# Low parts of the channel mixer's split weights: an adding DMA on the negated high part, in place of a subtraction on VectorE

## The chip, the cores and the metric

One core of one Trainium2 chip runs the whole program. The metric is the time of one execution in microseconds (us) of device time, lower is better. The engines are named as in the profile: PE (TensorE), with PEld for its weight loads, DVE (VectorE), ACT (ScalarE), POOL (GpSimd) and SP (SyncE), which starts most of the DMAs. The 16 DMA engines move the data of every queue.

## The reference, cut to what matters

The kernel computes one layer of a decoder for 512 prompt tokens and 8 x 8 sample tokens, T = 576 columns in all. Two token mixers (a chunked mLSTM and an RWKV-7 branch) come first, then the channel mixer, then a gated input per layer and the last norm. The change lies in the channel mixer's up projection and in the output of `y`:

```python
h2 = rmsnorm(x, lp['norm2_g'])
u = h2 @ lp['f_up']                                # (1024 -> 2 x 2816)
c, fconv_new = causal_dwconv(fconv, u[..., :D_FF], lp['f_conv_w'], lp['f_conv_b'])
x = x + (jax.nn.gelu(c) * u[..., D_FF:]) @ lp['f_down']

gate = jax.nn.sigmoid(rmsnorm(x, lp['ple_norm_g']) @ lp['ple_gate_w'])
x = x + gate * (pe.astype(x.dtype) @ lp['ple_proj'])
...
y_prompt = rmsnorm(y_p, final_norm_g)
```

All inputs are float32.

## The kernel before

Activations lie with 128 features on the partitions and the 576 tokens in the free dimension, in two halves of 288. A matmul takes a 128x128 weight tile and 128x288 activations. To keep more digits than one float32r pass has, every operand is split in a high part (the value rounded to float32r) and a low part (what is left), and a product is three matmuls: high x high, high x low, low x high. Weights come by DMA as float32 tiles `wr` of 128 x 4 x 128 (256 KB), ACT makes the high part `wh` by a cast (S.copy), and DVE the low part `wl` by a subtraction (wr - wh). For most weights this is done in `wload` (lines 166 and 167).

The up projection of the channel mixer has 22 blocks `j` of 128 gate features and 128 value features. The first three (`lead2`) go through `wload` and `dense`. The other 19 go through `up(j)` and `seven`, which treats gate and value rows, two halves of the inputs and two halves of the tokens as a 2x2 block product and does it with seven products in place of eight. `seven` loads four raw tiles (`wdma8`: a11, a21, a22, a12, in 6 rotating buffers `wr`), forms four sums of weights (`plus`: s1, s2, s4 on DVE, s3 on POOL, in 3 rotating buffers `ws`), and makes seven pairs of parts (`parts`, lines 287 to 290): of a11, s2, s1, a12, s3, a22 and s4. Each pair feeds one `prod` of 4 x 3 matmuls on PE (line 300). The pairs rotate in 4 buffers of `wh` and 4 of `wl`, which the other projections share. The combinations of the products, the convolution (L1333, L1335), the gelu (L1336) and the products with the value rows follow on DVE and ACT; POOL copies the last columns to `o_f` (L1326, L1327) and prepares the edges of `u`.

The blocks are done in three groups (`GR`): 8, 7 and 7 calls of `up`, after each of which comes a down projection of that group through `dense`; the first three calls of the first group are the `lead2` blocks. In front of the first group stands the second norm, whose parts `xb0` to `xb7` and combinations n1, n2, t3, n4 (`mixed`) feed all seven products.

At the end, for each half of the tokens, the last norm's eight products (L1403, tile `yo`) are written out in five pieces of 2, 2, 2, 1 and 1 tiles by SP (L1404). `yo` is one tile of 8 x 288 per half; tile `y` of the convolution, 592 wide, has two buffers.

The order of instructions on each engine is not written by hand: a scheduler of the framework places the instructions of all loops, and each engine then runs its own list in that order. An instruction whose input or buffer isn't ready holds up all that stands behind it on its engine. A new tile of a rotating set waits until the last reader of the one `bufs` turns earlier is done.

Of the kernel before, what the change touches and what calls it, by code (L numbers as in the profile page):

```python
# [7 lines left out]
F32 = mybir.dt.float32  # L8
F32R = mybir.dt.float32r
AF = mybir.ActivationFunctionType  # L10
ALU = mybir.AluOpType
# [4 lines left out]
P = 128  # L16
# [5 lines left out]
HF = T // 2  # L22
KD = D // P
# [69 lines left out]
def build(tc, nc, I, O):  # L93
    from contextlib import ExitStack

    V, S, G, TE, SY = nc.vector, nc.scalar, nc.gpsimd, nc.tensor, nc.sync
    st0 = ExitStack()

    def pool(stack, name, bufs=1, space=None, **kw):
        if space is not None:  # L100
            kw["space"] = space
        if space is None:
            kw["reuse_waits"] = "tile"
        return stack.enter_context(tc.tile_pool(name=name, bufs=bufs, **kw))

    with st0:
        cp = pool(st0, "const")
        wp = pool(st0, "wts")
# [6 lines left out]
        def bank(tag="m", name="pm"):  # L115
            if tag == "d" and turn:
                tag = turn[0]
                turn.append(turn.pop(0))
            return ps.tile([P, 512], F32, tag=tag, name=name, bufs=nbufs[tag])
# [5 lines left out]
        def vcol(name, k=0, rows=P):  # L125
            return vec[0:rows, VEC[name] + k:VEC[name] + k + 1]
# [15 lines left out]
        def wdma8(src, k):  # L142
            wr = wp.tile([P, 4, P], F32, tag="wr", name="wr", bufs=RB)
            SY.dma_start(wr, src[:, k:k + 4, :])
            return wr
# [10 lines left out]
        WB, RB = 4, 6  # L156
# [24 lines left out]
        def dense_half(pm, ws, xs, hf, ks=None):  # L181
            c = slice(hf * HF, (hf + 1) * HF)
            n = len(xs)
            for k in ks or range(n):
                half_k(pm, ws, xs[k], k, n, c)
# [52 lines left out]
        def add_squares(pl, acc, x, k, hf, eng=None, on_v=False):  # L238
            c = slice(hf * HF, (hf + 1) * HF)
            if k == 0:  # L240
                (eng or V).tensor_tensor(acc[:, c], x[:, c], x[:, c], ALU.mult)
            else:
                sq = pl.tile([P, HF], F32, tag="sq", name="sq", bufs=3)
                if on_v:
                    V.tensor_tensor(sq, x[:, c], x[:, c], ALU.mult)
                else:
                    S.activation(sq, x[:, c], AF.Square)  # L247
                (eng or V).tensor_tensor(acc[:, c], acc[:, c], sq, ALU.add)
# [19 lines left out]
        def mixed(tiles, pl, b11, b12, b21, b22, k, T4):  # L268
# [6 lines left out]
            for name, t, e in (("n2", n2, V), ("n1", n1, G), ("t3", t3, V), ("n4", n4, V)):  # L275
# [2 lines left out]
                e.tensor_tensor(l, t, h, ALU.subtract)  # L278
                T4[name].append((h, l))

        def seven(srca, srcb, x4, sp):

            def parts(w):
                wh, wl = [wp.tile([P, 4, P], F32R, tag=t, name=t, bufs=WB) for t in ("wh", "wl")]
                S.copy(wh, w)  # L288
                V.tensor_tensor(wl, w, wh, ALU.subtract)  # L289
                return wh, wl  # L290

            def plus(a, b, e):
                t = sp.tile([P, 4, P], F32, tag="ws", name="ws", bufs=3)
                e.tensor_tensor(t, a, b, ALU.add)  # L294
                return t

            def prod(pm, w, xs, more=False):
                for k in range(4):
                    for i, (a, b) in enumerate(((0, 0), (0, 1), (1, 0))):
                        TE.matmul(pm[:, 0:HF], w[a][:, k, :], xs[k][b], start=not more and k == 0 and i == 0,  # L300
                                  stop=k == 3 and i == 2, skip_group_check=more)

            def tile(tag):
                return sp.tile([P, HF], F32, tag=tag, name=tag, bufs=2)

            a11, a21, a22, a12 = wdma8(srca, 0), wdma8(srcb, 0), wdma8(srcb, 4), wdma8(srca, 4)
            A, F, E, Dm = (bank("d", "pd") for _ in range(4))
            w11 = parts(a11)
            prod(A, w11, x4["b11"])
            u3 = tile("u3")  # L310
            S.copy(u3, A[:, 0:HF])
            s1 = plus(a21, a22, V)
            s2 = plus(s1, a11, V)
            prod(F, parts(s2), x4["n2"])
            u2 = tile("u2")
            V.tensor_tensor(u2, F[:, 0:HF], u3, ALU.add)
            prod(E, parts(s1), x4["n1"])
            prod(A, parts(a12), x4["b21"], True)
            s3 = plus(a11, a21, G)
            prod(F, parts(s3), x4["t3"], True)  # L320
            V.tensor_tensor(u3, F[:, 0:HF], u3, ALU.add)
            prod(Dm, parts(a22), x4["n4"])
            s4 = plus(s2, a12, V)
            w4 = parts(s4)

            def last():
                prod(E, w4, x4["b22"], True)

            return A, u2, E, Dm, u3, last
# [887 lines left out]
        x1 = [rpool.tile([P, T], F32, name=f"res{m}") for m in range(8)]  # L1217
# [43 lines left out]
        with ExitStack() as stw:  # L1261
# [5 lines left out]
            for hf in range(2):  # L1267
                c = slice(hf * HF, (hf + 1) * HF)
# [17 lines left out]
        fp = pool(stf_, "ffn")  # L1286
# [63 lines left out]
        for g, (j0, nj) in enumerate(GR):  # L1350
# [8 lines left out]
            for m in range(8):  # L1359
                pss = dense(I["f_down"][m, :, j0:j0 + nj, :], acts)  # L1360
                for hf in range(2):
                    c = slice(hf * HF, (hf + 1) * HF)
# [26 lines left out]
        for hf in range(2):  # L1389
            c = slice(hf * HF, (hf + 1) * HF)  # L1390
            for m in range(8):
                pm = bank("d", "pd")
                dense_half(pm, wg[m], xs2, hf)
                th = fp.tile([P, HF], F32, tag="u", name="gth", bufs=2)
                S.activation(th, pm[:, 0:HF], AF.Tanh, scale=0.5)
                V.scalar_tensor_tensor(th, th, 1.0, pps[m][:, c], ALU.add, ALU.mult)
                V.scalar_tensor_tensor(x1[m][:, c], th, 0.5, x1[m][:, c], ALU.mult, ALU.add)
                add_squares(rpool, acc, x1[m], m, hf, on_v=m == KD - 1)
            rs = rms_half(rpool, acc, hf, "mr"[hf])
            yo = fp.tile([P, KD, HF], F32, tag="yo", name="yo")  # L1400
            for k0, n in ((0, 2), (2, 2), (4, 2), (6, 1), (7, 1)):
                for k in range(k0, k0 + n):
                    V.scalar_tensor_tensor(yo[:, k, :], x1[k][:, c], vcol("final_norm_g", k), rs, ALU.mult, ALU.mult)  # L1403
                SY.dma_start(O["o_y"][k0:k0 + n, :, c].rearrange("k p t -> p k t"), yo[:, k0:k0 + n, :])  # L1404

        for h in range(4):
            pc = bank("scsr"[h])
# [105 lines left out]
```

## Time and profile before

| | |
|---|---|
| median of 2 runs | 1105.82 us (1104.89 to 1106.75) |
| the profiled execution | 1105.56 us, its span 1103.9 us |
| PE | 1075.5 us busy, 97% |
| DVE | 785.3 us, 71% |
| ACT | 509.2 us, 46% |
| POOL | 254.6 us, 23% |
| DMA | 114.54 MB, mean 104 GB/s, share 34% |

The span is the time from the first to the last record of the profiled execution; what its own time has beyond that lies around it. A share of an engine is an average over stages with different limits: the calls of `up` lie in three runs between about 662 and 972 us of the span, with the down projections between them. In rows of groups the columns are the line, engine, operation, result and operands with shapes and types, how often, busy us and mean ns of one, and the idle time in front of them with what ended it. Rows of a stretch have the stretch, its length, busy us and count for PE, PEld, DVE, ACT and POOL, the granted clock, the share of the DMA engines and GB/s.

### The profile page before, as it was taken

The page shows a single profiled execution, that of the slowest core. Times are in us where ns is not written, and L with a number is a line of the kernel's source. Part 1 is how long each engine was busy: PE and PEld are TensorE (multiplying, and loading weights), DVE is VectorE, ACT ScalarE, POOL GpSimd, SP SyncE. Part 2 cuts the span into 40 slices and gives each one's busy share as a digit, 9 for nine tenths or more (in the row PEclk, how much of TensorE's full clock was granted, in tenths as well). Part 3 has the DMA queues.
Part 4 walks back from the last instruction along what each step waited for, and adds up shares of the span by engine and source line. Part 5 has one row for each costly group of instructions (what it writes and reads, how often), then busy time and mean ns, then how long its engine had stood idle before and what let it go on. Part 6 is the DMA issues. An engine that isn't in the chain of part 4 may idle for free. (4 is left out here: it accounts for less than half of the span.)

```text
span 1103.9 us, 23247 instructions
## 1 busy us (share of the span) xinstructions
PE 1075.5 (97%) x9039; PEld 1014.2 (92%) x9039; DVE 785.3 (71%) x1690; ACT 509.2 (46%) x1075; POOL 254.6 (23%) x401
## 2 busy tenths in 40 slices
PE   6899999999999999999989999999999999999997
PEld 5899989989979888898989999999999999999997
DVE  7786756766757667346693799974899569976765
ACT  6584733453435244325241556541455335553732
POOL 6532112220112022002130152410144103510300
PEclk9999999999999999999999999999999999999999
DMA  6343412332342232427780212332223332242414
GB/s 220 96 123 92 105 51 55 97 119 65 93 133 80 75 82 85 141 80 235 231 276 1 69 44 87 96 100 93 77 86 95 93 92 87 84 122 64 147 48 132
DMA packets 90799, 114.54 MB, mean 104 GB/s; under 512 B 35612, under 2 KB 45212, under 8 KB 90688
## 3 DMA queue, kind: packets, MB, share of 16 engines
q1 hardware_dynamic: 90688, 113.05, 34.2%
q8 instruction: 71, 1.16, 0.4%
q14 instruction: 40, 0.33, 0.1%
HBM read 94.57 MB, written 18.45 MB: 102 GB/s over the span
## 5 line engine op out<-in xcount | busy, mean ns | idle before, releaser
L166 ACT CAST wh<-wr 128x512 fp32r<-128x512 f32 (+2 forms) x170 | 101.6, 599 | 198.4 <-PE pd L190 157.3
L167 DVE TENSOR_TENSOR wl<-wr,wh 128x512 fp32r<-128x512 f32 (+2 forms) x170 | 119.7, 707 | 81.2 <-ACT wh L166 78.3
L190 PE MATMUL pd<-actl,wh 128*128 128x288 f32 x384 | 111.9, 295 | 0.0
L190 PE MATMUL pd<-acth,wl 128*128 128x288 f32 x384 | 111.4, 295 | 0.0
L190 PE MATMUL pd<-acth,wh 128*128 128x288 f32 x384 | 110.4, 296 | 0.5 <-ACT pp L1376 0.5
L190 PEld LDWEIGHTS pd<-acth,wh 128*128 128x128 f32 x384 | 71.1, 188 | 0.8 <-ACT pp L1376 0.7
L190 PEld LDWEIGHTS pd<-actl,wh 128*128 128x128 f32 x384 | 71.8, 188 | 0.0
L190 PEld LDWEIGHTS pd<-acth,wl 128*128 128x128 f32 x384 | 71.6, 188 | 0.0
L288 ACT CAST wh<-ws 128x512 fp32r<-128x512 f32 x76 | 47.0, 619 | 47.6 <-PE pd L300 26.8
L289 DVE TENSOR_TENSOR wl<-ws,wh 128x512 fp32r<-128x512 f32 x76 | 59.0, 777 | 8.2 <-ACT wh L288 7.9
L294 POOL TENSOR_TENSOR ws<-wr 128x512 f32<-128x512 f32 x19 | 31.9, 1682 | 93.6 <-DVE wl L289 53.1
L1326 POOL COPY o_f<-u 128x2 f32<-128x2 f32 x22 | 26.6, 1208 | 110.5 <-DVE u L1323 108.8
L288 ACT CAST wh<-wr 128x512 fp32r<-128x512 f32 x57 | 35.3, 619 | 35.0 <-PE pd L300 21.1
L289 DVE TENSOR_TENSOR wl<-wr,wh 128x512 fp32r<-128x512 f32 x57 | 39.6, 694 | 7.3 <-ACT wh L288 7.2
L1335 DVE SCALAR_TENSOR_TENSOR y<-u,vec,y 128x592 f32<-128x592 f32 x44 | 38.0, 863 | 1.4 <-ACT y L1333 1.3
L207 POOL TENSOR_TENSOR rsc<-rsc,nhalf 128x3 f32<-128x3 f32 x8 | 7.3, 912 | 137.0 <-DVE rsc L229 137.0
L247 ACT ACTIVATE sq<-res 128x288 f32<-128x288 f32 x40 | 17.7, 444 | 45.8 <-DVE res L1272 27.2
L190 PE MATMUL pd<-mgl,oh 128*128 128x288 f32 x112 | 33.1, 296 | 0.0
L190 PE MATMUL pd<-mgh,ol 128*128 128x288 f32 x112 | 33.1, 295 | 0.0
L190 PE MATMUL pd<-mgh,oh 128*128 128x288 f32 x112 | 32.8, 295 | 0.0
L1363 DVE TENSOR_TENSOR res<-res,pd 128x288 f32<-128x288 f32 x48 | 20.9, 451 | 15.6 <-PE pd L190 15.5
L190 PE MATMUL pd<-xa0h,wh 128*128 128x288 f32 x86 | 26.6, 310 | 2.1 <-ACT zr L346 2.0
(820 smaller groups left out, 3979.2 us busy)
## 6 DMA issues: line engine op xcount, KB each, us to landing
wr<-i_w_in SPq DMA_DIRECT2D x92, 256.0 KB
wr<-i_f_up SPq DMA_DIRECT2D x88, 256.0 KB
wr<-i_f_down SPq DMA_DIRECT2D x32, 256.0 KB
d_th<-gst SPq DMA_DIRECT2D x16, 288.0 KB
th<-d_th SPq DMA_DIRECT2D x16, 288.0 KB
wr<-i_w_br SPq DMA_DIRECT2D x16, 256.0 KB
wr<-i_w_out SPq DMA_DIRECT2D x16, 256.0 KB
wr<-i_ple_gate SPq DMA_DIRECT2D x16, 256.0 KB
```

Of the source, the lines that this page charges most:

```text
L166: S.copy(wh[:, 0:nk, :], wr[:, 0:nk, :])
L167: V.tensor_tensor(wl[:, 0:nk, :], wr[:, 0:nk, :], wh[:, 0:nk, :], ALU.subtract)
L190: TE.matmul(pm[:, 0:HF], w[:, k % 4, :], a[:, c], start=k == 0 and i == 0, stop=k == n - 1 and i == 2)
L207: G.tensor_tensor(t, t, nhalf[0:t.shape[0], :].to_broadcast([t.shape[0], n]), ALU.pow)
L247: S.activation(sq, x[:, c], AF.Square)
L288: S.copy(wh, w)
L289: V.tensor_tensor(wl, w, wh, ALU.subtract)
L294: e.tensor_tensor(t, a, b, ALU.add)
L1326: G.tensor_copy(o_f[:, j, 0:2], u[:, TP:TP + 2])
L1335: V.scalar_tensor_tensor(y, u[:, i:i + 592], w(i), y, ALU.mult, ALU.add)
L1363: V.tensor_tensor(x1[m][:, c], x1[m][:, c], pss[hf][:, 0:HF], ALU.add)
```

## The change

In `parts` the low part is no longer a subtraction on DVE. ACT writes the rounded value a second time, with its sign turned, into `wl` (an activation Copy with scale -1), and POOL then starts a DMA that adds the float32 source `w` to it in place: wl = -wh + w. Every third pair gets buffers of its own (`ph`, `pl`, two each, 8 KB of a partition), so that six pairs rotate. To make room, `yo` is cut into pieces of two tiles that rotate in the two buffers of `y`.

```diff
+        spare = [True, False, False]
+
         def seven(srca, srcb, x4, sp):
...
             def parts(w):
-                wh, wl = [wp.tile([P, 4, P], F32R, tag=t, name=t, bufs=WB) for t in ("wh", "wl")]
+                own = spare.pop(0)
+                spare.append(own)
+                wh, wl = [sp.tile([P, 4, P], F32R, tag=t, name=t, bufs=2) if own else
+                          wp.tile([P, 4, P], F32R, tag=t, name=t, bufs=WB) for t in (("ph", "pl") if own else ("wh", "wl"))]
                 S.copy(wh, w)
-                V.tensor_tensor(wl, w, wh, ALU.subtract)
+                S.activation(wl, w, AF.Copy, scale=-1.0)
+                G.dma_start(wl, w, accum_op=ALU.add)
                 return wh, wl
...
             rs = rms_half(rpool, acc, hf, "mr"[hf])
-            yo = fp.tile([P, KD, HF], F32, tag="yo", name="yo")
             for k0, n in ((0, 2), (2, 2), (4, 2), (6, 1), (7, 1)):
+                yo = fp.tile([P, 2, HF], F32, tag="y", name="yo", bufs=2)
                 for k in range(k0, k0 + n):
-                    V.scalar_tensor_tensor(yo[:, k, :], x1[k][:, c], vcol("final_norm_g", k), rs, ALU.mult, ALU.mult)
-                SY.dma_start(O["o_y"][k0:k0 + n, :, c].rearrange("k p t -> p k t"), yo[:, k0:k0 + n, :])
+                    V.scalar_tensor_tensor(yo[:, k - k0, :], x1[k][:, c], vcol("final_norm_g", k), rs, ALU.mult, ALU.mult)
+                SY.dma_start(O["o_y"][k0:k0 + n, :, c].rearrange("k p t -> p k t"), yo[:, 0:n, :])
```

The lines below `parts` stand 6 or 7 lines further down in the changed kernel: a cast of `parts` is L288 before and L294 now, `prod` is L300 and L307, the gelu L1336 and L1343. The instructions ahead of the channel mixer keep their order.

ACT, about one call of `up` from the last third of the channel mixer, from one gelu to the next; before:

```order
L1336 ACTIVATE y<-y 128x592
L288 CAST wh<-ws 128x512
L195 CAST acth<-ac 128x576
L288 CAST wh<-ws 128x512
L288 CAST wh<-wr 128x512
L311 COPY u_10334<-pd 128x288
L288 CAST wh<-ws 128x512
L288 CAST wh<-wr 128x512
L1333 ACTIVATE y<-u,vec 128x592
```

The same stretch now, cut where it has as many rows:

```order
L1343 ACTIVATE y<-y 128x592
L294 CAST wh<-ws 128x512
L1329 COPY u<-pd 128x288
L295 ACTIVATE wl<-ws 128x512
L294 CAST wh<-wr 128x512
L295 ACTIVATE wl<-wr 128x512
L195 CAST acth<-ac 128x576
L294 CAST ph<-ws 128x512
L295 ACTIVATE pl<-ws 128x512
L294 CAST wh<-wr 128x512
L318 COPY u_10551<-pd 128x288
L295 ACTIVATE wl<-wr 128x512
```

Behind nearly every cast stands its negated copy, so that the same copies out of PSUM (`u<-pd`) and the cast of `acth` stand between twice as many instructions of `parts`.

POOL, one call of `up` in the second run of calls; before, the sum s3 and the small copies are all that it has:

```order
L294 TENSOR_TENSOR ws<-wr 128x512
L1311 MEMSET u 128x2
L1313 COPY u<-stf 128x8x2
L1326 COPY o_f<-u 128x2
L1327 COPY o_f<-u 128x16
```

Now the adds stand between them, seven to a call (L301 is s3, L1333 and L1334 the copies to `o_f`):

```order
L301 TENSOR_TENSOR ws<-wr 128x512
L296 DMA wl<-ws 128x512
L296 DMA wl<-wr 128x512
L296 DMA pl<-ws 128x512
L296 DMA wl<-wr 128x512
L1333 COPY o_f<-u 128x2
L1334 COPY o_f<-u 128x16
L296 DMA wl<-ws 128x512
L296 DMA pl<-wr 128x512
L296 DMA wl<-ws 128x512
L1318 MEMSET u 128x2
L1320 COPY u<-stf 128x8x2
```

POOL's queue thus gains seven waits for ACT per call, and s3 and the copies of `o_f` stand behind them.

PE, where the first run of calls begins; before, the first product (L300, of `xb0` to `xb3`) stands behind all matmuls of the `lead2` blocks (L190):

```order
L190 MATMUL pd<-xb7h,wh 128x288
L190 MATMUL pd<-xb7l,wh 128x288
L190 MATMUL pd<-xb7h,wl 128x288
L300 MATMUL pd<-xb0h,wh 128x288
L300 MATMUL pd<-xb0l,wh 128x288
L300 MATMUL pd<-xb0h,wl 128x288
```

Now it starts some 80 rows earlier, ahead of the `lead2` matmuls that read `xb2` and `xb3`, the later parts of the norm:

```order
L307 MATMUL pd<-xb0h,ph 128x288
L307 MATMUL pd<-xb0l,ph 128x288
L307 MATMUL pd<-xb0h,pl 128x288
L307 MATMUL pd<-xb1h,ph 128x288
L190 MATMUL pd<-xb2l,wh 128x288
L190 MATMUL pd<-xb2h,wl 128x288
L190 MATMUL pd<-xb2l,wh 128x288
L190 MATMUL pd<-xb2h,wl 128x288
L307 MATMUL pd<-xb1l,ph 128x288
```

The low part `pl` of that product is read by PE before the `lead2` blocks are done. At the end of the program the order of the `yo` products and their DMAs of the second half is the same; only their waits for buffers are new.

## The prediction

> **What bounds the kernel now.** I read the page's busy shares first, then the busy time by stage, then who waited for whom, then the groups of the lines that the change touches. The first row sums one execution of 1105.56 us (its span is 1103.9 us, 1.66 us lie around it; the median of the runs shown is 1105.82 us, so one stands for the other). The two stretches are the middle of the second and third run of `up` calls; the columns are the stretch, its length, then busy time and instructions of PE, PEld, DVE, ACT and POOL, then the clock, the DMA engines' share and GB/s.
>
> ```profile
> PE 1075.5 (97%) x9039; PEld 1014.2 (92%) x9039; DVE 785.3 (71%) x1690; ACT 509.2 (46%) x1075; POOL 254.6 (23%) x401
> PE 42%; DVE 4%; DMA 1%; ACT 1%; issue 0%; POOL 0%; POOLq 0%; DVEq 0%; ACTq 0%
> 777.00:852.00 75.00, 75.00 (x568) 75.00 (x568) 71.47 (x133) 43.71 (x78) 29.36 (x28) 1.00 0.29 90
> 900.00:972.00 72.00, 72.00 (x546) 72.00 (x545) 69.00 (x129) 41.78 (x74) 26.85 (x27) 1.00 0.30 88
> PE pd L190 <- DVE xb2l L264: 1.2, 1, 1.2
> ...
> PE pd L190 <- POOL xb3l L264: 0.5, 1, 0.5
> ...
> PE pd L300 <- DVE wl L289: 0.4, 1, 0.4
> ```
>
> PE is the bound where the change acts: it is busy without a gap, at 75.00 us / 568 = 0.132 us from one matmul to the next. One `up` call has 7 products of 4 x 3 matmuls, 84 x 0.132 = **11.09 us**, and there are 19 such calls. DVE is nearly as full (71.47 of 75 us), yet PE waited for its low parts (`wl`) once, for 0.4 us. So the work taken off DVE frees an engine that is close to being late and is not late. What can be gained is small; the question is what the new path costs.
>
> **What the change removes and adds, per `up` call.** These are the groups of the three kinds of instruction (mean ns last before the idle time), and starts of neighbours, which show the pitch: durations overlap a little.
>
> ```profile
> L289 DVE TENSOR_TENSOR wl<-ws,wh 128x512 fp32r<-128x512 f32 x76 | 59.0, 777 | 8.2 <-ACT wh L288 7.9
> L289 DVE TENSOR_TENSOR wl<-wr,wh 128x512 fp32r<-128x512 f32 x57 | 39.6, 694 | 7.3 <-ACT wh L288 7.2
> 838.43 0.68 DVE L289 TENSOR_TENSOR wl<-wr,wh 128x512 fp32r<-128x512 f32 x1
> 839.03 0.68 DVE L289 TENSOR_TENSOR wl<-ws,wh 128x512 fp32r<-128x512 f32 x1
> 662.80 0.62 ACT L166 CAST wh<-wr 128x512 fp32r<-128x512 f32 x1
> 663.32 0.61 ACT L288 CAST wh<-wr 128x512 fp32r<-128x512 f32 x1
> L503 ACT ACTIVATE xk<-zr,dv 128x512 f32<-128x512 f32 x4 | 2.9, 718 | 1.4 <-DVE nkk L333 1.4
> ```
>
> *DVE* loses 7 subtractions at 0.60 us pitch, 4.2 us: from 71.47/75 x 11.09 = 10.6 to 6.4 us. Worth nothing on the path but the 0.4 us above.
> *ACT* gains 7 negated copies, one behind each cast. Before it works 43.71/75 x 11.09 = 6.5 us per call. At the cast's pitch of 0.52 us the sum is 10.1 us, which PE's 11.09 hides; at the 0.72 us of the dearest row of that shape (it scales by a vector) it is 11.5 us, 0.4 us too much, 8 us over 19 calls. I take the cast, which has the same operands but the factor: 0, with 8 kept as an end.
> *POOL* gains 7 DMA issues between its small copies and the sum `s3`. It works 29.36/75 x 11.09 = 4.3 us now, so 6.75 us are left, 0.96 us for each issue.
>
> ```profile
> L144 SPq DMA_DIRECT2D wr<-i_f_up x76: 327/328/427, 631.9 to 954.2; - x76
> L294 POOL TENSOR_TENSOR ws<-wr x19: 1287/1737/2428, 637.3 to 964.2; 128x512 f32<-128x512 f32 x19
> ```
>
> No DMA starts on POOL before, so the issue is bounded by SP's for the same tile, 0.33 us, and by the shortest pass of POOL itself over such a tile, 1.29 us. At 0.33 POOL comes to 6.6 us and is hidden; at 1.29 to 13.4 us, 2.3 us too long, 43 us over 19 calls. I take SP's, the same kind of work. The Trainium skill, page "DMA: Bandwidth & Descriptors", section "Latency and other measured facts", gives about 1 us to the first byte for a DMA issued from this engine, against 0.6 from SP. If POOL were held for all of that, my estimate from that figure is 11.3 us per call and 5 us in all; no run here shows it.
>
> *The DMA engines* are the term that decides. Each add moves one 128x512 tile: it reads `w`, reads the negated `wl`, and writes `wl`, so 256 KB are read twice. What they do at best is seen where they are fullest: 278 GB/s at a share of 0.84 in the first row, and 408 in the best slice of the second.
>
> ```profile
> 512.00:570.00 58.00, 54.80 (x380) 52.16 (x381) 44.58 (x73) 24.46 (x42) 13.06 (x10) 0.97 0.84 278
> GB/s 341 264 267 386 407 408 405 332 344 182 316 114 268 7 236 149 265 289 206 270 114 223 250 325 251 307 298 300 265 347 241 290 290 310 284 314 302 298 337 325
> wr<-i_f_up SPq DMA_DIRECT2D x88, 256.0 KB
> ```
>
> One pass of 262144 bytes takes 0.79 us at 278/0.84 = 331 GB/s, 0.64 us at 408. A call loads 4 tiles and adds 7. If an add costs two passes, that is (14 + 4) passes, 18 x 0.64 = 11.6 to 18 x 0.79 = 14.2 us; the middle is 12.9 us against PE's 11.09. **1.8 us too much per call**, x 19 = 34 us (10 to 59). Off this comes what is made ahead: the pairs `ph`, `pl` are used by no down projection, so before each of the three runs of calls 2 pairs can be filled, 3 x 2 x 1.43 us (two passes, middle) = 8.6 us. Left: **+25 us** (1 to 50). If an add cost one pass, 11 x 0.79 = 8.7 us fit beside PE, and the term is 0.
>
> I take two passes, from what the instruction must read. The Trainium skill speaks against the change in the same sense: "Collectives: The Full Stack", section "Part 3: Why 7× under link rate — side-by-side accounting", has a reducing DMA at half the rate of a copying one (32.35 against 62.28 GB/s), since it emits two read descriptors per chunk. By that rule my sum stands, without it the first rival does; no trace here shows it yet.
>
> **The parts at the two ends.** At the start of the first run PE waits 1.2 + 0.5 us for `xb2l` and `xb3l` of DVE and POOL. The new order puts a first product of `up(3)` ahead of those matmuls, so I count -1.7 us. At the end `yo` gets two buffers of two tiles in place of one of eight.
>
> ```profile
> 1096.90 3.49 DVE L1403 SCALAR_TENSOR_TENSOR yo<-res,vec,pm 128x288 f32<-128x288 f32 x8 [2.24 <-PE pm L235]
> 1097.86 1.23 SPq L1404 DMA_DIRECT2D o_y<-yo  x2
> ...
> 1099.73 1.44 SPq L1404 DMA_DIRECT2D o_y<-yo  x3
> 1.25 0.42 SPq L380 DMA_DIRECT2D x<-i_x  x1
> 3.91 1.28 ACT L404 ACT_TABLE_LOAD   x1 [3.91 <-DMA x<-i_x]
> ```
>
> The third piece now waits until the first has landed, and the fifth for the third. A transfer lands 3.91 - 1.25 = 2.66 us after its issue begins (first load of the program). First issue 1097.86, landed 1100.52; two products of 3.49/8 = 0.44 us, 1101.4; issue and landing, 1104.15; one product, 1104.6. The last issue was at 1100.8 and the span ended 3.1 us behind it; now it is at 1104.7, so the end moves by **+3.9 us** (2.5 to 5, by what 288 KB take over 144). DVE's same waits in the first half lie beside 8 x 24 x 0.132 = 25 us of PE's matmuls: 0.
>
> Sum: 1105.56 + 25.4 - 1.7 + 3.9 = **1133 us**.
>
> **Rivals.**
> *The adds are hidden* (an add costs near one pass, issue and landing fit). For it: the queues run at a share of 0.29 in the stage, and six pairs of parts in place of four give 6 x 1.585 = 9.5 us from one use of a pair to the next. Against it: two reads. PE stays the bound: 1105.56 - 1.7 + 3.9 = 1108 us, not slower by what can be told. It decides up to (11.09 - 4 x 0.79)/7 = 1.13 us of the engines per add. It could dip to 1104 if the tail's waits were covered as well.
>
> *The ring of `ws` or POOL's queue binds.* The 4 sums of a call share 3 buffers, and each is now held until its add has landed: sum 0.60, cast 0.52, negation 0.52, then L from POOL's turn to the landing; `s3` takes 1.1 us more on POOL. So (4 x (1.64 + L) + 1.1)/3 us per call, which passes 11.09 at L = 6.4 us. Transfers of 144 KB landed after 2.66 us; two passes of 0.64 to 0.79 us and a load between make 4.5 to 5.5 us, so the margin is an engine's single wait: POOL takes its DMAs in program order, and behind an add that waits for ACT stand the next adds, `s3` and the `o_f` copies. SP's loads wait for the raw tiles in the same way, already now:
>
> ```profile
> SPq L144 <- DVE wl L289: 92.9, 28, 9.1
> ```
>
> L = 8 us gives 13.2 us per call, +40 us; L = 10 gives 15.9, +91 us. POOL held for 1.29 us per issue gives +43 us. So 1148 to 1199 us with the two ends.
>
> *Faster by what can be told* would need 22 us. In the whole span PE idles 1103.9 - 1075.5 = 28 us, of which only the waits quoted, 2.1 us, lie where DVE is relieved.
>
> **How the numbers follow.** A measurement of this kernel tells about 2% (22 us) from no change. The DMA-bound forecast has 0.45, and runs from 1108 to 1158 us by its own ends; evenly spread, 0.6 of it lies above 1128. The hidden case has 0.27, the ring or POOL 0.27, a gain 0.01. Slower: 0.27 + 0.27 = 0.54; within 2%: 0.18 + 0.27 = 0.45; faster: 0.01. The range runs from the hidden case's low end, 1104, to 1180 us; past that lies only the upper part of the ring's case. Likeliest alone: 1108 to 1158.
>
> **What would show it.** DVE's share in the runs of calls falls to about 0.6 and ACT's rises to 0.8 or more; if ACT shows no idle time its pitch was wrong. The DMA share there goes from 0.3 to over 0.9 if two passes are paid, to about 0.8 if one. PE then has gaps in the runs of calls and none in the down projections, and waits for adds (`wl`, `pl`) and not for DVE. If the gaps are there while the DMA share stays under 0.8, it is the ring or POOL: then ACT and DVE wait for `ws`, or POOL is busy to the end. The last `yo` products show waits for `o_y`. I am wrong outright if PE keeps 0.132 us per matmul through these stretches, or if POOL is held for several us by one issue.

## The result, and the profile after

The changed kernel takes **1166.68 us** (1166.02 to 1167.34), 1.055 times the time before (95% interval 1.0504 to 1.0596): 60.9 us more, where 27 more were forecast. The profiled execution took 1166.02 us, its span is 1164.3 us. The page of the changed kernel, first the busy shares, then the two large DMA queues (q1 is SP's, q0 is POOL's: packets, MB, share of 16 engines' span), then the chain that ended last:

```profile
PE 1094.0 (94%) x9039; PEld 1021.3 (88%) x9039; DVE 710.1 (61%) x1557; ACT 575.0 (49%) x1208; POOL 324.1 (28%) x534
q1 hardware_dynamic: 90688, 113.05, 32.4%
q0 software_dynamic: 19152, 34.87, 17.4%
PE 26%; DMA 9%; issue 6%; DVE 4%; POOL 4%; ACT 2%; POOLq 0%; DVEq 0%; ACTq 0%
```

DVE has lost 75 us and ACT has gained 66, as the change meant it. PE's share of the chain fell from 42% to 26%, and DMA's rose from 1% to 9%. PE's idle time grew from 28 us to 70 (1164.3 - 1094.0), so 42 us of the 60 are gaps; the other 18 are busy time with the same 9039 matmuls, a small part of it at a lower clock (last section).

The same two stretches as before follow. The changed kernel runs later, so both also hold a piece of a down projection (from 900 to 920 us no matmul is one of `up`), and their DMA shares of 0.84 and 0.68 are not those of the calls alone. After them comes one of 60 us in which the changed kernel's PE does nothing but products of `up` (of before, then of after); columns as in the prediction:

```profile
777.00:852.00 75.00, 66.77 (x475) 64.45 (x473) 31.14 (x63) 45.75 (x85) 34.51 (x48) 0.98 0.84 172
900.00:972.00 72.00, 67.35 (x490) 66.07 (x489) 31.67 (x64) 36.54 (x66) 23.38 (x33) 0.98 0.68 148
```

```profile
800.00:860.00 60.00, 60.00 (x455) 60.00 (x454) 58.27 (x113) 34.86 (x61) 26.14 (x26) 1.00 0.30 92
```

```profile
800.00:860.00 60.00, 51.77 (x361) 49.45 (x361) 27.60 (x56) 40.54 (x75) 32.70 (x48) 0.97 0.95 193
```

PE did 361 matmuls where it did 455. A call of 84 matmuls takes 84 x 60/361 = 13.96 us there, against 11.08. None of the engines that compute is full (the busiest, PE, has 51.77 of 60 us); the DMA engines' share is 0.95. Of the waits in the runs of calls (us in all, times, longest), those of PE, of DVE and of ACT on this path:

```profile
DVE ws L301 <- DMA wl<-ws: 51.9, 18, 6.8
...
ACT wh L294 <- DVE ws L301: 23.1, 13, 4.2
...
DVE ws L301 <- DMA pl<-ws: 19.0, 8, 5.3
...
PE pd L307 <- DMA wl<-wr: 17.1, 15, 2.4
...
PE pd L307 <- DMA wl<-ws: 9.9, 8, 2.2
...
PE pd L307 <- DMA pl<-wr: 6.1, 8, 1.3
...
PE pd L307 <- DMA pl<-ws: 2.9, 2, 1.8
```

PE waits for adds, 36 us in 33 waits, and no more for DVE's low parts. The lines above them show a second thing: DVE waits 71 us before the sums (L301), because a buffer of `ws` is free only when the add that reads it has landed. SP's loads wait in the same way for the adds that read raw tiles, 219 us in the runs of calls. ACT waits for DVE in turn, and the next add is issued late. So the signs of two cases of the prediction stand in one trace: full DMA engines, and a ring that is held. Which of them costs the time is what the experiments had to say.

The groups of the new instructions on POOL and ACT, and the adds' landing (256 KB each, median us from issue to landing):

```profile
L296 POOL DMA_DIRECT2D wl<-ws x51 | 47.7, 940 | 42.4 <-ACT wl L295 25.4
...
L295 ACT ACTIVATE wl<-ws 128x512 fp32r<-128x512 f32 x51 | 32.0, 628 | 0.0
...
wl<-ws POOLq DMA_DIRECT2D x51, 256.0 KB, 4.8
```

### The profile page after: what moved, and what is told of

Same layout as the page of the kernel before. It is cut to its first block, busy times and chain, and to the rows that moved or that the text cites. A ratio compares the mean times of both kernels' runs of the same rounds, so it can differ in the third digit from the quotient of the medians.

```text
span 1164.3 us, 23625 instructions
## 1 busy us (share of the span) xinstructions
PE 1094.0 (94%) x9039; PEld 1021.3 (88%) x9039; DVE 710.1 (61%) x1557; ACT 575.0 (49%) x1208; POOL 324.1 (28%) x534
## 3 DMA queue, kind: packets, MB, share of 16 engines
q0 software_dynamic: 19152, 34.87, 17.4%
## 4 chain that ended last, share of the span: by engine, by line
PE 26%; DMA 9%; issue 6%; DVE 4%; POOL 4%; ACT 2%; POOLq 0%; DVEq 0%; ACTq 0%
PE pd L190 20%; PE pd L307 5%; DMA wl<-ws 4%; DMA pl<-ws 2%; DMA wl<-wr 2%; POOL wl L296 1%; POOL pl L296 1%; DMA wr<-i_f_up 1%; DVE xnf L262 1%; DVE ws L301 1%; POOL ws L301 1%; DMA pl<-wr 1%; ACT wl L295 0%; DVE y L1342 0%; DMA o_y<-yo 0%
## 5 line engine op out<-in xcount | busy, mean ns | idle before, releaser
L190 PE MATMUL pd<-actl,wh 128*128 128x288 f32 x384 | 112.2, 294 | 0.0
L190 PE MATMUL pd<-acth,wh 128*128 128x288 f32 x384 | 111.3, 296 | 0.4 <-ACT pp L1383 0.4
L190 PE MATMUL pd<-acth,wl 128*128 128x288 f32 x384 | 111.6, 295 | 0.0
L301 DVE TENSOR_TENSOR ws<-ws,wr 128x512 f32<-128x512 f32 x38 | 28.0, 737 | 83.1 <-DMA wl<-ws 51.9
L190 PEld LDWEIGHTS pd<-acth,wh 128*128 128x128 f32 x384 | 71.4, 188 | 0.7 <-ACT pp L1383 0.6
L190 PEld LDWEIGHTS pd<-actl,wh 128*128 128x128 f32 x384 | 71.9, 188 | 0.0
L190 PEld LDWEIGHTS pd<-acth,wl 128*128 128x128 f32 x384 | 71.6, 188 | 0.0
L296 POOL DMA_DIRECT2D wl<-ws x51 | 47.7, 940 | 42.4 <-ACT wl L295 25.4
L294 ACT CAST wh<-ws 128x512 fp32r<-128x512 f32 x51 | 31.4, 616 | 42.6 <-DVE ws L301 23.1
L296 POOL DMA_DIRECT2D wl<-wr x37 | 34.1, 927 | 35.1 <-ACT wl L295 11.3
L301 POOL TENSOR_TENSOR ws<-wr 128x512 f32<-128x512 f32 x19 | 26.8, 1413 | 43.4 <-DMA wr<-i_f_up 22.6
L190 PE MATMUL pd<-mgl,oh 128*128 128x288 f32 x112 | 33.1, 295 | 0.0
L190 PE MATMUL pd<-mgh,ol 128*128 128x288 f32 x112 | 33.1, 295 | 0.0
L190 PE MATMUL pd<-mgh,oh 128*128 128x288 f32 x112 | 32.8, 295 | 0.0
L295 ACT ACTIVATE wl<-ws 128x512 fp32r<-128x512 f32 x51 | 32.0, 628 | 0.0
L296 POOL DMA_DIRECT2D pl<-ws x25 | 24.4, 975 | 25.3 <-ACT pl L295 14.3
```

The lines of the kernel that those rows point to most:

```text
L190: TE.matmul(pm[:, 0:HF], w[:, k % 4, :], a[:, c], start=k == 0 and i == 0, stop=k == n - 1 and i == 2)
L295: S.activation(wl, w, AF.Copy, scale=-1.0)
L296: G.dma_start(wl, w, accum_op=ALU.add)
```

## The experiments

All kernels start from the changed one unless it is said otherwise, and each ratio is to the kernel before on the same chip. The scheduler places the instructions of each kernel anew. By the traces, ACT, DVE and POOL run the same lists in the changed kernel and e2, in e3 and e10, and in e4 and e8; in the other pairs compared below the order differs too, and what that alone is worth was not measured. Where buffers were added (e3, e5, e9, e10, e11), the room comes from one buffer less of `xnf`, `sq` and `rsb`, which the norms use. e2, e10 and e12 leave out the addition, e11 leaves out three quarters of it, and e13 and e14 add the high part in place of the source, so that the low part is lost.

| run | adds per call | data per add | source held | `ws` | median us | ratio (95%) |
|---|---|---|---|---|---|---|
| after | 7 | two passes | yes | 3 | 1166.7 | 1.055 (1.0504 to 1.0596) |
| e1_ws_only | 4, of the sums | two passes | yes | 3 | 1152.8 | 1.0417 (1.038 to 1.0454) |
| e2_copy | 7 | one pass | yes | 3 | 1120.6 | 1.0133 (1.0099 to 1.0168) |
| e3_ws5 | 7 | two passes | yes | 5 | 1159.9 | 1.0489 (1.0457 to 1.0521) |
| e4_six_pairs | none | - | no | 3 | 1108.7 | 1.0032 (1.0007 to 1.0057) |
| e5_ws_only_ws5 | 4, of the sums | two passes | yes | 5 | 1125.8 | 1.0163 (1.0131 to 1.0195) |
| e6_raw_only | 3, of raw tiles | two passes | yes | 3 | 1119.8 | 1.0116 (1.0084 to 1.0148) |
| e7_third_tail | every third | two passes | yes | 3 | 1121.3 | 1.0114 (1.0081 to 1.0148) |
| e8_six_pairs_tail | none | - | no | 3 | 1107.5 | 1.0007 (0.999 to 1.0024) |
| e9_raw_wr8 | 3, of raw tiles | two passes | yes | 3 | 1113.8 | 1.0058 (1.0037 to 1.0079) |
| e10_copy_ws5 | 7 | one pass | yes | 5 | 1117.5 | 1.0097 (1.0075 to 1.0118) |
| e11_quarter_ws5 | 7 | a quarter | yes | 5 | 1126.1 | 1.0161 (1.0132 to 1.019) |
| e12_negation_alone | none | - | no | 3 | 1108.0 | 1.0017 (1.0001 to 1.0034) |
| e13_add_reads_wh | 7 | two passes | no | 3 | 1144.9 | 1.0352 (1.0326 to 1.0377) |
| e14_quarter_reads_wh | 7 | a quarter | no | 3 | 1116.2 | 1.0086 (1.0064 to 1.0107) |

### Capacity or ring: e1 to e4

Theory A: the DMA engines have too little capacity for seven adds of two passes. Theory B: the ring of three `ws` buffers, each held to the landing, sets the pace. e1 adds only for tiles that are sums and subtracts the raw ones on DVE, which takes three adds of seven off the DMA engines and leaves the ring as it is (`sums` holds what `plus` has returned).

```diff
-                S.activation(wl, w, AF.Copy, scale=-1.0)
-                G.dma_start(wl, w, accum_op=ALU.add)
+                if any(w is t for t in sums):
+                    S.activation(wl, w, AF.Copy, scale=-1.0)
+                    G.dma_start(wl, w, accum_op=ALU.add)
+                else:
+                    V.tensor_tensor(wl, w, wh, ALU.subtract)
```

> Only the four sums s1 to s4 of a call get their low parts by an adding DMA; those of the three raw tiles are subtracted on DVE again. Theory A (the DMA engines' capacity): a call then asks 4 x 1.45 + 4 x 0.83 = 9.1 us of the DMA engines, less than PE's 11.09, so the loss goes: about 1110 us. Theory B (the ring of three ws buffers, each held until its add has landed): all four ring tiles still wait for an add, so most of the loss stays: with the effective 8.6 us from cast to landing shortened by 1 us for the lighter load, (7.66 + 4 x 7.6)/3 = 12.7 us per call, about 1140 us.

Measured: 1152.8 us, above even B's 1140. In the trace of e1, the stretch of 60 us, then POOL's queue in it (packets, MB, share) and DVE's waits in the runs of calls:

```profile
800.00:860.00 60.00, 50.38 (x355) 49.40 (x354) 38.72 (x73) 35.30 (x65) 23.20 (x37) 0.94 0.71 156
```

```profile
q0 software_dynamic: 2685, 4.88, 46.7%
```

```profile
DVE ws L306 <- DMA wl<-ws: 36.8, 15, 5.5
DVE ws L306 <- DMA pl<-ws: 28.9, 7, 4.9
```

The DMA engines are free for 0.29 of the time, and a call still takes 84 x 60/355 = 14.2 us, with DVE in front of its sums for 66 us in the runs of calls. The ring limits here by itself; A as the only cause is out. A part of e1's time is clock: PE's gaps are longer (up to 4.6 us), and from 660 to 1040 us the granted clock is 0.96 on average, against 0.99 in the changed kernel and 1.00 before; at PE's pace that is some 0.04 x 380 = 15 us (an estimate). e2 changes the other one: a DMA that copies, so one pass in place of two.

```diff
-                G.dma_start(wl, w, accum_op=ALU.add)
+                G.dma_start(wl, w)
```

> The DMA of parts copies w over the low part in place of adding it (the low parts are then w itself; left out is the add). Same issues on POOL, same waits, one read in place of two. Theory A: 7 x 0.75 + 4 x 0.83 = 8.6 us per call, hidden by PE: about 1110 us, share of the DMA engines in the calls about 0.75. Theory B: a landing is only shortened by the second pass and the shorter queue, some 1 to 1.5 us of 8.6: about 12.5 us per call, 1130 to 1140 us.

Measured: 1120.6 us, between the two theories. Of the 61 us, 46 go when the add becomes a copy, under the same ring and with the same order of instructions: the second pass goes, and a copy also lands sooner and holds POOL a shorter time, so the ring turns faster too. The copy's queue in the stretch of 60 us, its issue on POOL (ns, min, median, max), and its landing:

```profile
q0 software_dynamic: 5210, 9.49, 50.4%
```

```profile
L296 POOL DMA_DIRECT2D wl<-ws x51: 527/528/577, 670.1 to 982.2; - x51
...
DMA to landing us min/median/max: 2.2/3.8/5.8
```

e3 gives the changed kernel five `ws`.

```diff
-                t = sp.tile([P, 4, P], F32, tag="ws", name="ws", bufs=3)
+                t = sp.tile([P, 4, P], F32, tag="ws", name="ws", bufs=5)
```

> As the changed kernel, with 5 buffers of ws in place of 3 (room made by one xnf, one sq and one rsb buffer less, used in the norms only). Theory A: the engines still need 7 x 1.45 + 4 x 0.83 = 13.5 us per call against PE's 11.09, so at best 10 us of the 60 come back: about 1155 us. Theory B: (7.66 + 4 x 8.6)/5 = 8.4 us per call, hidden: about 1110 us.

Measured: 1159.9 us, 5 above A's number and far from B's. In the trace of e3 the queue's share and DVE's waits in front of the sums:

```profile
q0 software_dynamic: 4082, 7.44, 72.5%
```

```profile
DVE ws L301 <- DMA wr<-i_f_up: 52.1, 19, 4.7
DVE ws L301 <- DMA wl<-ws: 45.5, 14, 5.3
```

The DMA engines are as full as in the changed kernel, and DVE now also waits for raw tiles: their ring of six `wr` is held by adds too (SP's loads wait for such adds, 211 us in the runs of calls). Neither of the two limits alone explains the 61 us, and lifting one alone can show little while the other stands (7 us here, 15 in e1). e4 takes the adds out and keeps six pairs and the cut `yo`, with the subtraction back on DVE.

> As the changed kernel with six pairs of buffers and the cut yo, but the low part subtracted on DVE as before: no adding DMA, no negated copy. Both theories: no loss in the calls. What is left is the tail of yo (+3.9 us forecast) and a first product started earlier (-1.7): 1106 to 1110 us.

Measured: 1108.7 us. The pairs and the tail cost 3.5 us together (1.0032); the rest hangs on the adds.

### Both lifted in part: e5 to e8

Theory C: capacity and ring, and nothing else. Theory D: each add lands late, and engines that run a fixed order meet that whatever the buffers. e5 is e1 with five `ws`, e6 adds only for the three raw tiles, e7 only for every third pair, and e8 for none; e7 and e8 put `yo` of the second half in tiles of their own, which undoes the tail.

```diff
+                if hf:
+                    if k0 in (0, 4):
+                        yx = fp.tile([P, 4, HF], F32, tag="x4", name="yo", bufs=8)
+                    yo = yx[:, k0 % 4:k0 % 4 + n, :]
+                else:
+                    yo = fp.tile([P, 2, HF], F32, tag="y", name="yo", bufs=2)
```

> Adding DMAs for the four sums only, and 5 buffers of ws: the two edits of e1 and e3 together. Each of them alone left most of the loss. Theory C (two limits of about 14 us per call that cover each other: the DMA engines' capacity with seven adds, the ring of three ws tiles with any adds on them): with both lifted the calls go back to PE's 11.09 us, about 1110 us, and DVE waits little for adds. Theory D (neither; an add lands 4.5 to 5 us behind its issue, and engines that work in program order stand still behind each one): the landing is as late as in e1, so the time stays near e1's, 1140 to 1153 us.

> Adding DMAs for the three raw tiles only, the four sums subtracted on DVE; 3 ws buffers. No ws tile waits for an add, and the engines have 3 x 1.45 + 4 x 0.83 = 7.7 us of work per call. Theory C: neither limit holds: about 1109 us (the tail's 3.5 us). Theory D: three late landings per call in place of four in e1, so about 3/4 of e1's loss: 1135 to 1142 us.

> An add for every third pair only (those in the buffers ph and pl), the others subtracted on DVE; and in the second half of the tokens yo lies in tiles that the gate's weights have left, so that its products wait for no transfer. Theory C: engines 2.33 x 1.45 + 3.3 = 6.7 us per call, a ring tile in 4 of 7 of the adds: hidden or nearly; with the tail back at before's, 1103 to 1107 us. Theory D: 2.33 late landings per call: 1125 to 1135 us.

> No adds, no negated copies: six pairs of buffers with the subtraction on DVE, and the second half of yo in tiles that wait for no transfer. Both theories: the tail's 3.5 us of e4 come back, and what is left of the change is the first product started earlier (forecast 1.7 us): 1103 to 1106 us.

Measured: 1125.8, 1119.8, 1121.3 and 1107.5 us. Two more buffers take 28 us off e1 (1.0417 to 1.0163), which is the ring, with what the clock loses behind its gaps. But e5, e6 and e7 all stay about 11 us or more above what C says, at DMA engines that are not full (0.79, 0.69 and 0.60 in the stretch of 60 us); they also stay under D's numbers. Both fell. e8 against e4 prices the tail: 1.0032 - 1.0007 = 0.0025, 2.8 us, with an uncertainty of about 3. e8 itself came out 1.5 us above its forecast. In e6, DVE waits in front of sums for raw tiles that are not yet loaded:

```profile
DVE ws L306 <- DMA wr<-i_f_up: 19.3, 14, 3.2
```

### What is left besides capacity: e9 to e12

e9 is e6 with eight raw buffers in place of six.

```diff
-        WB, RB = 4, 6
+        WB, RB = 4, 8
```

> Adds for the three raw tiles of a call only, the four sums subtracted on DVE, and 8 rotating raw buffers `wr` in place of 6 (room by one buffer less of `xnf`, `sq` and `rsb`). The same with 6 raw buffers took 1119.8 us, 9.5 us above the tail's 1108.7 and the reference run's noise; DVE waited there 14 times, 19.3 us, in front of sums for raw tiles that had not been loaded. Theory E (an added tile keeps its raw buffer until the add has landed, so the loads come late): with 8 buffers those waits go and the time is 1107 to 1112 us. Theory D (each add lands 4 to 5 us after its issue, and engines that run in a fixed order meet that by chance, whatever the number of buffers): 1116 to 1121 us.

Measured: 1113.8 us, between the two. The longer ring of raw tiles takes 6 us (1.0116 to 1.0058) off a cost of some 10 beside the tail's, and DVE's wait for raw tiles falls from 19.3 us to 4.7; holding the sources is a real part, not all. e10 is the copy with five `ws`, e11 adds one slice of four with five `ws`, and e12 has no DMA in `parts` at all.

```diff
-                G.dma_start(wl, w, accum_op=ALU.add)
+                G.dma_start(wl[:, 0:1, :], w[:, 0:1, :], accum_op=ALU.add)
```

> The changed kernel with a copying DMA in place of the adding one (the addition is left out: wl becomes w) and 5 rotating buffers `ws` in place of 3. All seven issues of POOL and all waits stay; an issue moves one pass of 256 KB in place of two, and lands after 3.8 us in place of 4.9. With 3 buffers the copy took 1120.6 us, the adding kernel with 5 buffers 1159.9. Theory C (two limits of about the same size, the capacity of the DMA engines and the ring of `ws`): with both lifted 1106 to 1111 us. Theory D (late landing against a fixed order on the engines remains): 1116 to 1121 us.

> The changed kernel with 5 buffers `ws` and each add over one of the four slices of a tile (128x128 of 128x512; three quarters of the addition are left out). Seven issues, seven waits and the order stay; the data of a call's adds falls from 7 x 1.45 = 10.2 us of the DMA engines to a quarter, 2.5 us, and the share of the engines in the runs of calls should fall from 0.95 to about 0.5. Theory C (capacity and ring, nothing else): 1106 to 1110 us. Theory F (the issue of an accumulating DMA on POOL, 0.9 us, or its fixed latency, costs time whatever its size): 1115 to 1130 us, with waits on the adds about as many as with the copy.

> The changed kernel without any DMA of `parts`: ACT writes the negated high part and nothing is added (the low part is left out). DVE is relieved, ACT has its seven negations, POOL no issue, six pairs, cut `yo`. It prices ACT's part. If ACT's work is hidden as the prediction had it (10.1 us per call beside 11.09): 1105 to 1110 us, the tail's +2.8 us included. If ACT's pitch is too long: 1112 to 1118 us, with PE waiting for ACT's `wl` in the runs of calls.

Measured: 1117.5 us, which is D's and not C's: two more `ws` take 4 us off the 15 that the copy costs with three, by intervals that overlap. 1126.1 us, which is F's. And 1108.0 us, as hidden work has it. e12, the two stretches of before:

```profile
777.00:852.00 75.00, 75.00 (x568) 75.00 (x567) 43.98 (x94) 64.07 (x121) 11.45 (x30) 1.00 0.31 92
900.00:972.00 72.00, 72.00 (x545) 72.00 (x544) 41.73 (x87) 61.89 (x117) 10.91 (x28) 1.00 0.31 93
```

PE has no gap: ACT's seven negations are hidden entirely, at 64.07 of 75 us busy. e11 is the surprise. In its stretch of 60 us:

```profile
800.00:860.00 60.00, 53.41 (x379) 51.66 (x378) 33.53 (x66) 44.95 (x86) 35.57 (x54) 0.97 0.57 111
```

The DMA engines have 0.43 of the time free, and PE still does 379 matmuls, not 455. The size of an add is not what costs 18 us over e12. POOL is held 0.87 us per issue (median) as for a full tile, but is busy only 35.57 of 60 us. Beside e10, which has the same `ws` and holds its sources too, e11 moves a quarter of the data and lands as soon (median 3.2 us from the issue, against 3.3), and still takes 7 us more (1.0161 against 1.0097). So neither the data nor the landing is what makes it dearer than a copy. POOL's hold of 0.87 us in place of 0.53 is one candidate; the order of the instructions, which differs, is the other.

### Are the sources the cost: e13 and e14

Theory R: what is left comes from the sources `ws` and `wr`, held until an add has landed. Theory F: POOL's issue, or the pair that is ready some 3 us later, costs PE by itself. Both runs let the add read `wh` in place of `w`, so that no source is held; e13 moves the whole tile, e14 a quarter.

```diff
-                G.dma_start(wl, w, accum_op=ALU.add)
+                G.dma_start(wl, wh, accum_op=ALU.add)
```

> The changed kernel with 3 buffers `ws`, in which the add reads the high part `wh` in place of the source `w` (so the true low part is left out: wl becomes 0). Each add still moves two passes of 256 KB, with seven issues of POOL, but the source tiles `ws` and `wr` are free as soon as ACT has read them. Theory C (capacity binds by itself, the rings are only a cover of about the same size): 1140 to 1155 us, the share of the DMA engines in the runs of calls at 0.9 or more. Theory R (the held sources are most of it): 1115 to 1130 us, the share at 0.85 or less.

> The same with each add over one of the four slices only: 3 buffers `ws`, no source tile held, a quarter of the data, seven issues of 0.87 us on POOL and a landing after about 3 us remain. With the source `w` and 5 buffers this took 1126.1 us. Theory R (held source tiles make the rest): 1107 to 1111 us. Theory F (POOL's issue, or the pair that is ready 3 us later, costs PE by itself): 1118 to 1127 us, with PE waiting for adds as often as before.

Measured: 1144.9 us, inside C's range, and 1116.2 us, between the two theories. The stretch of 60 us and the two queues in it for e13, then the stretch for e14:

```profile
800.00:860.00 60.00, 53.63 (x387) 52.70 (x386) 35.84 (x69) 46.53 (x87) 38.69 (x57) 0.97 1.04 217
```

```profile
q0 software_dynamic: 4442, 8.08, 77.5%
q1 hardware_dynamic: 2734, 4.85, 26.2%
```

```profile
800.00:860.00 60.00, 58.89 (x438) 57.89 (x437) 37.99 (x78) 49.58 (x93) 39.65 (x60) 1.00 0.63 122
```

In e13 the DMA engines are full, at a share of 1.04 (packets of two queues overlap), and a call takes 84 x 60/387 = 13.0 us. Against the changed kernel (361 matmuls, share 0.95) the hold on the sources is gone, and 22 us go with it; the order of the instructions differs too. e14 has the engines at 0.63 and is 84 x 60/438 = 11.5 us per call. e11, with sources held, five `ws` and the same data, had 13.3 in its stretch, which holds a gap of 3.6 us; over the whole program it is 8 us slower than e14 (1.0161 against 1.0086).

So the way from before to after can be walked in four steps, each the difference of two ratios times 1105.8 us: six pairs, the tail and ACT's negations (e12) +1.9; seven small adds, no source held (e14) +7.6; all their data (e13) +29.4; the sources held (after) +21.9. That makes 60.8 us. Each step is uncertain by 3 or 4 us, the last by 6, since only two executions of the changed kernel itself were timed. The steps are not independent: with capacity at its limit a late pair is hidden in part, and in another order of steps the shares would differ. The order of the instructions differs at each step as well. Not separated is what the 7.6 us consist of: POOL's issue, the landing, or the order that the scheduler chose.

The step of 29.4 us is not the DMA engines' capacity alone either, for the traces show a third limit: **at most three adds are in flight**. In the five kernels with seven adds per call (the changed one, e3, e11, e13 and e14; 133 adds each) no add starts before 0.31 us after the landing of the third add before it. In the changed kernel 46 of the 133 start within 0.4 us of that moment, though their tile had been negated, and POOL stands idle for 49 us in all in front of these; in e13 it is 75 adds and 64 us. At a median landing of 5.0 us, seven adds cannot take less than about 7 x 5.3/3 = 12.4 us per call (an estimate from these numbers), close to the 13.0 of e13. The copies do not meet this limit: when one starts, up to four others are in flight in e2, and up to three in e10. So full DMA engines and a short queue cannot be told apart in e13; what is shown is that the data of the adds costs this time, by one of them or by both.

## Why the prediction was right and wrong, point by point

**What bounds the kernel** was right. PE was the bound, DVE's relief was worth nothing (e4 and e8 with the subtraction are as fast as e12 without it), and no run came out faster than before.

**An add costs two passes**: right, within what the packets show. An add makes 19152/133 = 144 packets. In the stretch of 60 us the changed kernel's adds took this share (16 engines), and SP's queue this one:

```profile
q0 software_dynamic: 4128, 7.51, 72.7%
q1 hardware_dynamic: 2187, 3.99, 22.0%
```

That is 0.727 x 60 x 16/4128 = 0.169 us per packet, against 0.504 x 60 x 16/5210 = 0.093 for the copy of e2: 1.8 times. An add costs 9 packets per engine x 0.169 = 1.52 us, 0.76 a pass, within the 0.64 to 0.79 and above the middle. The Trainium skill, "Collectives: The Full Stack", section "Part 3: Why 7× under link rate — side-by-side accounting", has a reducing transfer at half the rate of a copying one for its second read; the 1.8 here comes near it.

**The term of capacity** came out well in size: 12.9 us per call were forecast, the engines' own time in e13 is (0.775 + 0.262) x 60 x 84/387 = 13.5 us, and the pace there 13.0; +25 us with the pairs made ahead, +29.4 as the step from e14 to e13. That the two agree so closely is in part luck: the queue of three sets nearly the same pace in e13, and the 8.6 us taken off for pairs made ahead were not tested.

**The ring of `ws` as a rival** is the step that failed: the sum put the hold on the sources, and POOL's queue, at 0. The prediction chose between capacity and ring, as if one of the two decided; here each sets a pace slower than PE's without the other (13.0 us per call in e13, 14.2 in e1, in the stretch of 60 us), and over the whole program both together cost more than either (61 us, against 39 in e13 and 46 in e1). The hold on the sources is worth **+22 us** by e13, with what the other order of instructions does in it. The sum was 33 us short: these 22, the 8 of e14 that it had at 0 (POOL's issue, the landing or the order) and 4 of the data's term. The time itself, 1166.7 us, lies in what the prediction gave for this rival (1148 to 1199 us), and its L = 8 us had +40.

The threshold was worked out from the landing alone, forecast at 4.5 to 5.5 us and measured at 4.8 to 5.1, in place of the whole time that a source is held. A call of 13.96 us asks for L = (3 x 13.96 - 1.1)/4 - 1.64 = 8.6 us by the prediction's formula. From the end of the negation to the landing, the adds of the changed kernel take 6.4 us on average, 1.5 of it before the issue, which the prediction named as a margin of "an engine's single wait" and left out of the sum. The other 2 us lie ahead of that, or between a landing and the next sum; they were not traced. One of the longest such chains of the changed kernel, ACT's negations and POOL's adds (start us, length, engine, in brackets what it waited for by the trace):

```profile
820.64 0.63 ACT L295 ACTIVATE wl<-wr 128x512 fp32r<-128x512 f32 x1
...
821.93 0.63 ACT L295 ACTIVATE wl<-ws 128x512 fp32r<-128x512 f32 x1
...
825.01 0.89 POOL L296 DMA_DIRECT2D wl<-wr  x1 [2.54 <-ACT pl L295]
...
826.70 0.87 POOL L296 DMA_DIRECT2D wl<-ws  x1 [0.81 <-issue]
```

The tile `wl<-ws` was negated by 822.56, and its add was issued at 826.70, 4.1 us later, with the landing still before it. Ahead of it in POOL's queue stood the add of a raw tile, whose negation had ended at 821.27 and which still went out only at 825.01, after 2.5 us of idle POOL. The ACT instruction that the trace names there belongs to the tile after; the landings show what POOL stood for:

| add started at | landed at | the third add behind it started at |
|---|---|---|
| 819.57 | 824.69 | 825.01 |
| 820.33 | 826.39 | 826.70 |
| 820.87 | 827.65 | 827.96 |

Three adds were in flight, and each further one went out 0.31 us after the first of the three had landed.

The raw tiles' ring was named in the prediction only as SP's wait; e3, e6 and e9 show that it counts as well.

**ACT at 0**: right, by e12. The negation lasts 0.628 us as the cast does, and the pitch of 0.52 holds.

**POOL at 0** rested on a wrong number, and does not hold. An issue holds POOL for 0.87 us (median) in place of SP's 0.33, and 0.94 on average for the group shown. POOL is still not full (32.70 of 60 us), but its queue stands still while three adds are in flight. The page "DMA: Bandwidth & Descriptors" of the Trainium skill, section "Latency and other measured facts", gives about 1 us to the first byte for such a DMA; the 0.87 us that an add holds POOL is near that, and not near SP's issue; the 0.53 of a copy is not. The +7.6 us of e14 are what this term, the late landing and the order cost together.

**The two ends.** The tail was forecast at +3.9 us (its terms add up to 0.1 us less) and is +2.8. The last `yo` products of the changed kernel:

```profile
1154.48 1.79 DVE L1410 SCALAR_TENSOR_TENSOR yo<-res,vec,pm 128x288 f32<-128x288 f32 x4 [2.24 <-PE pm L235]
1155.44 1.23 SPq L1411 DMA_DIRECT2D o_y<-yo  x2
1157.74 1.41 DVE L1410 SCALAR_TENSOR_TENSOR yo<-res,vec,pm 128x288 f32<-128x288 f32 x3 [1.48 <-DMA o_y<-yo]
...
1161.01 0.51 DVE L1410 SCALAR_TENSOR_TENSOR yo<-res,vec,pm 128x288 f32<-128x288 f32 x1 [1.86 <-DMA o_y<-yo]
```

The waits are where they were expected, twice on `o_y`; from the first product to the end of the span are 9.8 us in place of 7.0, which is the +2.8. The first transfer lands 1157.74 - 1155.44 = 2.3 us after its issue, not 2.66. The hoisted product at the start was forecast at -1.7 us; no gain shows (e8, which has six pairs and no tail, is at 1.0007).

**The signs** held in the main: waits for adds, gaps in the runs of calls and none in the down projections (PE is busy for all of 740 to 780 and 900 to 940 us), a share of over 0.9 in the calls. DVE's and ACT's shares were forecast for PE's full pace, about 0.6 and 0.8; at the slower pace they are 0.46 and 0.68 in the stretch of 60 us, and e12 at full pace has 0.59 and 0.85. But the sign that was to tell the cases apart ("If the gaps are there while the DMA share stays under 0.8, it is the ring or POOL") knew no case with both, and the share of 0.95 would have named capacity alone.

## What to carry to other kernels

A transfer that reads a tile for an engine holds that tile's buffer until it has landed: count the ring of the *source* as well as that of the result, and count the time from the tile's making through every in-order engine before the issue, not the landing alone. Count also how many transfers a queue keeps in flight: the time to landing, divided by that number, is a pace of its own. Where two limits stand at about the same pace, price both instead of choosing one, and lift both in an experiment, since lifting one alone can show little (7 us of 61 in e3). And work taken off an engine that nobody waits for is worth nothing, however full it looks (here 71.47 of 75 us).

## What the runs showed of the hardware that was not expected

*The price of an issue on POOL hangs on the kind of DMA, not on its size*: 0.87 us for an add of 256 KB (e13) and of 64 KB alike (e14; both are 128 rows), 0.53 for a copy of 256 KB (e2). The adds of e13, then those of e14 (ns: min, median, max):

```profile
L296 POOL DMA_DIRECT2D wl<-wh x88: 859/869/1791, 667.6 to 1003.2; - x88
```

```profile
L296 POOL DMA_DIRECT2D wl<-wh x88: 859/877/2152, 669.8 to 978.9; - x88
```

*POOL's queue kept at most three adds in flight, of 256 KB and of 64 KB alike.* The next one started 0.31 us after the landing of the third before it, at the earliest, in all five kernels with seven adds per call; copies of the same tile were up to five in flight (e2). This is no more than these kernels show: what the limit counts was not tested.

*A short gap of PE can cost clock behind it.* In e6, per us (columns as above, the clock is the third value from the end):

```profile
839.00:840.00 1.00, 0.05 (x1) 0.00 (x0) 1.00 (x2) 1.00 (x3) 0.98 (x3) 1.00 1.11 225
840.00:841.00 1.00, 0.00 (x0) 0.00 (x0) 1.00 (x3) 0.45 (x1) 0.82 (x2) 1.00 0.99 178
841.00:842.00 1.00, 0.79 (x3) 0.79 (x4) 1.00 (x4) 0.00 (x0) 0.41 (x1) 0.57 0.88 152
842.00:843.00 1.00, 1.00 (x6) 1.00 (x5) 0.44 (x3) 0.00 (x0) 0.00 (x0) 0.50 1.09 174
843.00:844.00 1.00, 1.00 (x6) 1.00 (x5) 0.00 (x0) 0.15 (x1) 0.00 (x0) 0.50 1.03 238
844.00:845.00 1.00, 1.00 (x7) 1.00 (x7) 0.48 (x2) 1.00 (x2) 0.00 (x0) 0.72 1.00 338
```

PE stood still for about 2.2 us, and then ran at a clock of 0.50 to 0.57 for some 3 us, 6 matmuls to the us in place of 7.6. The Trainium skill, "TensorE: Matmul & The Clock Gate", section "HAM oscillation — how this bites in real kernels", warns of gaps over about 3.4 us; here a gap of 2.2 us was followed by the lower clock. Not every such gap was: in the changed kernel PE stood still for 2.3 us from 686.8 us on, and the clock stayed at 1.00. This is part of why PE is busy longer in the changed kernel with the same matmuls, and a small one: from 660 to 1040 us its mean clock is 0.99, before 1.00, some 4 us of the 18 (an estimate); where the rest lies was not traced.
